# Query weights through four buffers, and a triangle inversion in 64-column blocks

## The chip, the cores and the metric

One core of a Trainium2 chip runs the kernel; the metric is the time of one execution on the device, in microseconds. The core has TensorE (PE; its weight loads are listed as PEld), VectorE (DVE), ScalarE (ACT), GpSimd (POOL) and SyncE (SP), each with its own queue of instructions that it works off in order; they wait for one another by semaphores. SyncE and GpSimd issue the DMAs.

## The reference, cut to what matters

One inference step of a one-layer decoder for two groups of tokens that share all weights: a prompt of 512 tokens and 8 samples of 8 tokens. All is float32.

```python
h = rmsnorm(x, g1) * (1 + sc1) + sh1          # the shifts and gates are silu(c) @ w_ada
proj = h @ w_in                               # 1024 -> 512 (S5) + 1792 (RWKV-7)
y_s5 = s5_mixer(proj[..., :512])              # diagonal state space, gelu, gated
y_rw = rwkv7_mixer(proj[..., 512:])           # 8 heads of 64: S = S*w - (S kk) (kk*a)^T + v k^T, y = S r
x = x + ga1 * (concat(y_s5, y_rw) @ w_out)
h = rmsnorm(x, g2) * (1 + sc2) + sh2
q = h @ w_q                                   # 8 heads of two halves of 64
s1, s2 = q_1 . keys1, q_2 . keys2             # 128 scores per half
idx, gate = softmax over the top 16 of (top 16 of s1) + (top 16 of s2)
ff = sum_k gate_k * gelu(u_tab[idx_k] . h) * v_tab[idx_k]    # 16384 experts, 128 per token
y = rmsnorm(x + ga2 * ff)
```

The recurrence of the RWKV part is computed in chunks of 64 tokens. Within a chunk that needs the inverse of a unit triangular 64 x 64 matrix for each head (8 x 8 blocks for the samples).

## The kernel before

Tokens are cut into five tiles: tile 0 holds the 64 sample tokens, tiles 1 to 4 hold 128 prompt tokens each, and they are worked in the order 1, 2, 3, 0, 4 (ORDER). Every tile passes through these stages, each of them a Python generator:

- front: the elementwise part of the RWKV mixer and the inversion. A prompt tile has two chunks of 64 tokens, a chunk 8 heads; heads lie in pairs, one on partitions 0 to 63 and one on 64 to 127. For each chunk, LT holds four such pairs as 128 x 128 matrices whose off-diagonal blocks are zero. The inverse grows by doubling: Dm and DT (the inverse and its transpose) begin as identities; on each of five levels TensorE forms LT x Dm (L1029), ScalarE evicts it (L1031), TensorE multiplies it with DT in two ways (L1037, L1041), and VectorE copies the blocks of that level into Dm and DT under a mask (L1042, L1043; masks in lev).
- back: the chunk recurrence with state S0, and the group norm.
- select: output projection with w_out (8 loads, L1230, matmuls L1232), norm, query projection with w_q (8 loads of 512 KB, one per head, L1270, matmuls L1272), and the products with the keys (loads L1276, matmuls L1286 and L1288). All these weights and two rows of modulation (ga1, sh2) go through one pool tag, "w", of two buffers.
- pick: the top 16 on VectorE (L1308 to L1312 on scores, L1335 to L1339 on candidates). For tiles 1, 2 and 3 (DENSE) it ends with three transposes on TensorE that put the chosen indices and gates into dib and dix (L1381 to L1385).
- gbuild, for the three dense tiles: 32 "quads" of four tokens each make one-hot factors (oh L1490 and ab L1497 on VectorE, ab L1494, L1495, L1500 on ScalarE, ab L1502 on GpSimd), multiply them (L1505), and ScalarE evicts the result into Gst (L1506). After four quads Gst is stored to Gd in HBM.

After all that comes the dense part: 128 blocks, each of a first product (pd, L1520, 24 matmuls) of 128 experts' u rows with 384 tokens, gelu, a multiplication with the gates Gr that are read back from Gd (wf, L1603), and a second product with the v rows (po, L1623, 18 matmuls). Beside it GpSimd gathers u and v rows for the tokens of tiles 0 and 4 (L1448), and VectorE reduces them.

Before all stands phase 1, the input projection and the S5 mixer; its end, with the rest of the conditioning product (ada, matmuls L303), is woven with the front of tile 1. Generators are advanced in turn (weave), and a scheduler then sets the order on each engine from priorities and its own estimate of times, so an edit in one stage can move instructions of all. The dense part's first loads are held until the last keys have been issued (kld).

Of the kernel before, what the change touches and what calls it, by code (L numbers as in the profile page):

```python
# [6 lines left out]
F32 = mybir.dt.float32  # L7
I32 = mybir.dt.int32
U32 = mybir.dt.uint32
U8 = mybir.dt.uint8  # L10
# [32 lines left out]
def layout(x):  # L43
# [60 lines left out]
    out["lev"] = np.stack(lv, 1).astype(np.float32)  # L104
# [73 lines left out]
class Kernel:  # L178
# [13 lines left out]
    B2 = {"r": 7, "l": 8, "b": 7, "s": 5}  # L192
# [658 lines left out]
    def open_rwkv(self):  # L851
# [11 lines left out]
        lev = wp.tile([128, 12, 128], U8)  # L863
# [21 lines left out]
        self.LTs = []  # L885
        for i in range(2):
            lt = wp.tile([128, 4, 128], F32, name="lt%d" % i)
            G.memset(lt, 0.0)
            self.LTs.append(lt)
        for q in range(0, 12, 6):  # L890
            lf = self.t4([6, 128])
            SY.dma_start(lf, I["lev"][:, q:q + 6])
            G.tensor_copy(lev[:, q:q + 6], lf)
# [12 lines left out]
    def front(self, ti):  # L906
# [84 lines left out]
        id4 = ident[:, None, :].to_broadcast([128, 4, 128])  # L991
        yield

        def lm(i):
            return self.lev[:, i, None, :].to_broadcast([128, 4, 128])
        cd = []
        for c in range(nch):
            gp = [ps([128, 4, 128], "r"), ps([128, 4, 128], "r")]
            for j in range(4):
                for hf in range(2):  # L1000
                    sl = slice(64 * hf, 64 * hf + 64)
                    T.matmul(gp[hf][:, j, :], BK[sl, c, j, :], AR[sl, c, j, :], start=True, stop=True)
            MG = t4([2, 4, 128])
            LT = self.LTs[c]
            for hf in range(2):
                sl = slice(64 * hf, 64 * hf + 64)
                V.tensor_tensor(MG[:, hf], gp[hf], gm[:, None, :].to_broadcast([128, 4, 128]), op=OP.mult)
                {"G": G.tensor_copy, "V": V.tensor_copy, "S": S.copy}[self.LTE[hf]](LT[sl, :, sl], MG[sl, hf, :, 0:64])
                gl = G.tensor_copy(MG[sl, hf, :, 0:64], AR[sl, c, :, 0:64])
            Dm = t2([4, 128])  # L1010
            DT = t2([4, 128], "l")
            S.copy(Dm, id4)
            S.copy(DT, id4)
            cd.append((MG, LT, Dm, DT))
            yield
        for MG, LT, Dm, DT in cd:
            pl = ps([128, 4, 128], "r")
            for j in range(4):
                T.transpose(pl[:, j, :], LT[:, j, :], ident)
            V.copy_predicated(Dm, lm(0), pl)  # L1020
            V.copy_predicated(DT, lm(1), LT)
        yield
        nl = 3 if smp else 6
        for l in range(1, nl):
            Bs = []
            for MG, LT, Dm, DT in cd:
                pb = ps([128, 4, 128], "r")
                for j in range(4):
                    T.matmul(pb[:, j, :], LT[:, j, :], Dm[:, j, :], start=True, stop=True)  # L1029
                Bm = t2([4, 128])  # L1030
                S.copy(Bm, pb)  # L1031
                Bs.append(Bm)
            yield
            for (MG, LT, Dm, DT), Bm in zip(cd, Bs):
                p2 = ps([128, 4, 128], "r")
                for j in range(4):
                    T.matmul(p2[:, j, :], Bm[:, j, :], DT[:, j, :], start=True, stop=True)  # L1037
                if l < nl - 1:
                    p1 = ps([128, 4, 128], "r")
                    for j in range(4):  # L1040
# [5 lines left out]
        self.rs[ti] = (AR, BK, [(MG, DT) for MG, LT, Dm, DT in cd], rk, vS, WL, gs)  # L1046

    def back(self, ti):
# [37 lines left out]
        for c in range(nch):  # L1086
            (MG, DT), (UV, BN) = cd[c], ub[c]
# [39 lines left out]
            for j in range(4):  # L1127
                T.matmul(pu[:, j, :], DT[:, j, :], Xs[:, j, :], start=True, stop=True)
# [75 lines left out]
    def select(self, ti):  # L1204
# [30 lines left out]
        ga1 = self.ws.tile([128, D], F32, name="ga1", tag="w", bufs=2)  # L1235
        self.mod(ga1, 0, smp)
        sh2 = self.ws.tile([128, D], F32, name="sh2", tag="w", bufs=2)
# [37 lines left out]
        keys = self.ws.tile([128, 8, 128], F32, name="keys", tag="w", bufs=2)  # L1275
# [463 lines left out]
```

## Time and profile before

| | |
|---|---|
| time, median of 3 runs (lowest, highest) | 1947.14 us (1943.68, 1952.03) |
| the profiled execution's own time | 1944.17 us |
| its span | 1942.4 us, 30575 instructions |
| TensorE | 1815.2 us busy (93%), 11183 matmuls |
| VectorE | 1533.6 us (79%) |
| ScalarE | 817.1 us (42%) |
| GpSimd | 676.0 us (35%) |
| mean granted clock of TensorE | 0.974 |
| DMA | 514.09 MB, mean 265 GB/s |

The shares are means over stages with different limits. The dense part fills the span from about 850 us on, with TensorE full; before it, up to that point, the stages of different tiles lie beside each other and the limit changes every 50 us or so. Times in the rows below are microseconds from the start of the span.

### The profile page before, as it was taken

The numbers are of one execution on the slowest core, as the hardware profiler recorded it, in microseconds if no ns is written. First come the engines' busy times: TensorE is split into PE (matmuls) and PEld (weight loads), VectorE is DVE, ScalarE is ACT, GpSimd is POOL, SyncE is SP. The second block draws the span as 40 slices with busy tenths as digits, with TensorE's granted clock in tenths as the row PEclk, the third lists the DMA queues.
The fourth block names the chain that finished last, engine by engine and source line by source line (L and its number), as shares of the span: only waits on it lengthen the run. The fifth ranks groups of instructions, "written<-read, shape, count | busy, mean of one in ns | idle before, by whom it ended". The sixth has DMA issues, their size and how long they took to land.

```text
span 1942.4 us, 30575 instructions
## 1 busy us (share of the span) xinstructions
PE 1815.2 (93%) x11183; PEld 1573.6 (81%) x11183; DVE 1533.6 (79%) x3117; ACT 817.1 (42%) x1494; POOL 676.0 (35%) x543
## 2 busy tenths in 40 slices
PE   8899998999979888689999999999999999999994
PEld 6699666877759686679999988899999999999993
DVE  7968435478797979399988877798888878888998
ACT  4232515525765788434333333433333333333332
POOL 0000201001262244313454434365444444544555
PEclk9899999989999999899999999999999999999998
DMA  8524653434345576789899998899999999999995
GB/s 330 152 86 103 220 181 104 142 123 152 126 163 185 190 255 241 282 281 311 299 372 354 351 348 321 272 383 352 341 350 321 349 337 344 331 343 349 326 316 200
DMA packets 203366, 514.09 MB, mean 265 GB/s; under 512 B 26248, under 2 KB 88840, under 8 KB 199120
## 3 DMA queue, kind: packets, MB, share of 16 engines
q1 hardware_dynamic: 147632, 309.74, 46.2%
q0 software_dynamic: 55584, 202.40, 28.7%
q8 instruction: 88, 1.44, 0.3%
q14 instruction: 62, 0.51, 0.1%
HBM read 471.28 MB, written 39.62 MB: 263 GB/s over the span
## 4 chain that ended last, share of the span: by engine, by line
PE 68%; DVE 13%; DMA 6%; ACT 5%; issue 5%; POOL 3%; SPq 0%; POOLq 0%; DVEq 0%; ACTq 0%
PE po L1623 23%; PE pd L1520 23%; PE par L329 4%; POOL gr L1448 3%; PE pas L1272 2%; DMA wq<-w_q 2%; PE par L1029 2%; PE par L1037 1%; PE pag L303 1%; PE pas L1232 1%; PE par L1041 1%; DVE oh L1490 1%; DMA gr<-v_tab,ei 1%; DVE idxu L1309 1%; PE pas L792 1%
## 5 line engine op out<-in xcount | busy, mean ns | idle before, releaser
L1448 POOL DMA_INDIRECT gr<-u_tab,ei x192 | 246.4, 1284 | 310.3 <-DVE scr L1453 256.7
L1448 POOL DMA_INDIRECT gr<-v_tab,ei x192 | 255.4, 1330 | 275.7 <-DVE acc L1463 240.3
L1520 PE MATMUL pd<-dh,uh 128*128 128x384 f32 x1024 | 344.7, 337 | 4.0 <-ACT wf L1601 3.1
L1520 PE MATMUL pd<-dh,ul 128*128 128x384 f32 x1024 | 344.8, 337 | 2.2 <-DVE ul L1517 2.2
L1520 PE MATMUL pd<-dl,uh 128*128 128x384 f32 x1024 | 343.6, 336 | 0.0
L1463 DVE SCALAR_TENSOR_TENSOR acc<-gr,act,acc 128x1024 f32<-128x1024 f32 x190 | 245.3, 1291 | 4.2 <-DMA gr<-v_tab,ei 2.4
L1516 ACT CAST uh<-ur 128x1024 fp32r<-128x1024 f32 x128 | 134.5, 1051 | 269.7 <-PE pd L1520 265.2
L1623 PE MATMUL po<-vl,wh 128*128 128x512 f32 x768 | 237.3, 391 | 1.2 <-DVE vl L1619 1.2
L1623 PE MATMUL po<-vh,wl 128*128 128x512 f32 x768 | 236.6, 390 | 0.0
L1453 DVE SCALAR_TENSOR_TENSOR scr<-gr,h 128x1024 bf16<-128x1024 f32 x192 | 233.8, 1218 | 1.3 <-DMA gr<-u_tab,ei 0.2
L1606 ACT CAST wh<-wf 128x384 fp32r<-128x384 f32 x128 | 65.9, 515 | 334.6 <-PE po L1623 310.8
L1623 PE MATMUL po<-vh,wh 128*128 128x512 f32 x768 | 200.3, 396 | 4.9 <-ACT vh L1618 4.4
L1517 DVE TENSOR_TENSOR ul<-ur,uh 128x1024 fp32r<-128x1024 f32 x128 | 156.4, 1222 | 61.4 <-ACT uh L1516 61.2
L1520 PEld LDWEIGHTS pd<-dh,uh 128*128 128x128 f32 x1024 | 192.7, 188 | 12.1 <-ACT wf L1601 4.9
L1520 PEld LDWEIGHTS pd<-dl,uh 128*128 128x128 f32 x1024 | 192.7, 188 | 5.2
L1520 PEld LDWEIGHTS pd<-dh,ul 128*128 128x128 f32 x1024 | 192.6, 188 | 3.7 <-DVE ul L1517 3.4
L1619 DVE TENSOR_TENSOR vl<-vr,vh 128x1024 fp32r<-128x1024 f32 x128 | 156.2, 1220 | 21.4 <-ACT vh L1618 21.3
L1623 PEld LDWEIGHTS po<-vl,wh 128*128 128x128 f32 x768 | 143.8, 188 | 32.6 <-DVE vl L1619 2.1
L1623 PEld LDWEIGHTS po<-vh,wl 128*128 128x128 f32 x768 | 144.1, 188 | 31.5 <-DVE wl L1607 0.4
L1623 PEld LDWEIGHTS po<-vh,wh 128*128 128x128 f32 x768 | 141.0, 188 | 33.4 <-ACT vh L1618 10.0
L1618 ACT CAST vh<-vr 128x1024 fp32r<-128x1024 f32 x128 | 134.5, 1051 | 46.7 <-PE po L1623 34.8
L1502 POOL TENSOR_TENSOR ab<-oh,dix 128x512 f32<-128x512 bf16 x72 | 88.2, 1230 | 150.2 <-DVE oh L1490 65.7
(472 smaller groups left out, 3135.8 us busy)
## 6 DMA issues: line engine op xcount, KB each, us to landing
ur<-u_t SPq DMA_DIRECT2D x128, 512.0 KB, 6.8
vr<-v_tab SPq DMA_DIRECT2D x128, 512.0 KB, 6.4
Gd<-Gst SPq DMA_DIRECT2D x24, 1024.0 KB, 4.8
Gr<-Gd SPq DMA_DIRECT2D x16, 1536.0 KB, 17.2
wo<-w_out SPq DMA_DIRECT2D x40, 512.0 KB, 4.5
wq<-w_q SPq DMA_DIRECT2D x40, 512.0 KB, 4.3
wt<-w_ada SPq DMA_DIRECT2D x32, 512.0 KB, 4.4
wr<-w_in SPq DMA_DIRECT2D x18, 512.0 KB, 6.7
```

Source lines behind the costliest of these rows:

```text
L329: mm = self.nc.tensor.matmul(p, w[:, k, :], h[:, k, c:c + 288], start=(k == 0 and i == 0), stop=(k == KB - 1 and i == 2))
L1448: G.indirect_dma_start(out=r, out_offset=None, in_=I[tab], in_offset=bass.IndirectOffsetOnAxis(ap=ei[:, k:k + 1], axis=0))
L1453: V.scalar_tensor_tensor(scr, r, 1.0, h2, op0=OP.mult, op1=OP.mult, accum_out=act[:, k:k + 1])
L1463: V.scalar_tensor_tensor(acc, r, act[:, k:k + 1], acc, op0=OP.mult, op1=OP.add)
L1502: G.tensor_tensor(A, oh, bc(self.dix[:, 1]), op=OP.mult)
L1516: nc.scalar.copy(uh, ur)
L1517: self.mark = nc.vector.tensor_tensor(ul, ur, uh.bitcast(F32), op=OP.subtract).ins
L1520: nc.tensor.matmul(pa, u[:, k, :], h[:, k, :], start=(k == 0 and i == 0), stop=(k == KB - 1 and i == 2))
L1606: S.copy(wh, wf)
L1618: S.copy(vh, vr)
L1619: V.tensor_tensor(vl, vr, vh.bitcast(F32), op=OP.subtract)
L1623: T.matmul(outs[2 * d + n], w[:, d * 128:(d + 1) * 128], v[:, n * 512:(n + 1) * 512], start=(b == 0 and i == 0), stop=(b == 127 and i == 2))
```

## The change

All of w_out, ga1, sh2, w_q and the keys get four buffers (tag "w", bufs=4). The room comes from the inversion, which no longer works on 128 x 128 matrices with zero blocks but on the 64 x 64 blocks alone, stacked on the two halves of the partitions: LT is one tile [128, 2, 4, 64] in place of two of [128, 4, 128], the masks lev are 64 columns wide, and the pool t2l has 6 buffers in place of 8. Both chunks of a prompt tile now go through each step together: one step is 16 products of 64 x 64 (8 for the samples), one eviction and one masked copy of [128, 8, 64].

```diff
-    B2 = {"r": 7, "l": 8, "b": 7, "s": 5}
+    B2 = {"r": 7, "l": 6, "b": 7, "s": 5}
...
-        lev = wp.tile([128, 12, 128], U8)
+        lev = wp.tile([128, 12, 64], U8)
...
-        for i in range(2):
-            lt = wp.tile([128, 4, 128], F32, name="lt%d" % i)
-            G.memset(lt, 0.0)
-            self.LTs.append(lt)
...
+        self.LT = wp.tile([128, 2, 4, 64], F32, name="LT")
...
+        def quads(out, a, b):
+            for u in range(m):
+                for hf in range(2):
+                    sl = slice(64 * hf, 64 * hf + 64)
+                    T.matmul(out[sl, u, :], a[sl, u, :], b(sl, u), start=True, stop=True)
...
         for l in range(1, nl):
-            Bs = []
-            for MG, LT, Dm, DT in cd:
-                pb = ps([128, 4, 128], "r")
-                for j in range(4):
-                    T.matmul(pb[:, j, :], LT[:, j, :], Dm[:, j, :], start=True, stop=True)
-                Bm = t2([4, 128])
-                S.copy(Bm, pb)
-                Bs.append(Bm)
-            yield
-            for (MG, LT, Dm, DT), Bm in zip(cd, Bs):
-                p2 = ps([128, 4, 128], "r")
-                for j in range(4):
-                    T.matmul(p2[:, j, :], Bm[:, j, :], DT[:, j, :], start=True, stop=True)
-                if l < nl - 1:
-                    p1 = ps([128, 4, 128], "r")
-                    for j in range(4):
-                        T.matmul(p1[:, j, :], DT[:, j, :], Bm[:, j, :], start=True, stop=True)
-                    V.copy_predicated(Dm, lm(2 * l), p1)
-                V.copy_predicated(DT, lm(2 * l + 1), p2)
+            pb = ps([128, m, 64], "r")
+            quads(pb, LT, lambda sl, u: Dm[sl, u, :])
+            Bm = t2([m, 64])
+            S.copy(Bm, pb)
+            yield
+            if l < nl - 1:
+                p1 = ps([128, m, 64], "r")
+                quads(p1, DT, lambda sl, u: Bm[sl, u, :])
+                V.copy_predicated(Dm, lm(2 * l), p1)
+            p2 = ps([128, m, 64], "r")
+            quads(p2, Bm, lambda sl, u: DT[sl, u, :])
+            V.copy_predicated(DT, lm(2 * l + 1), p2)
             yield
...
-                T.matmul(pu[:, j, :], DT[:, j, :], Xs[:, j, :], start=True, stop=True)
+                for hf in range(2):
+                    sl = slice(64 * hf, 64 * hf + 64)
+                    T.matmul(pu[sl, j, :], DT[sl, j, :], Xs[sl, j, :], start=True, stop=True)
...
-            wo = self.ws.tile([128, D], F32, name="wo", tag="w", bufs=2)
+            wo = self.ws.tile([128, D], F32, name="wo", tag="w", bufs=4)
...
-                wq = self.ws.tile([128, KB, 128], F32, name="wq", tag="w", bufs=2)
+                wq = self.ws.tile([128, KB, 128], F32, name="wq", tag="w", bufs=4)
```

(ga1, sh2 and the keys likewise.) The order of instructions changes on every engine. TensorE, one and a half levels of the inversion of tile 4, before (t2r and t2l are Dm, DT and the evicted product; wq are the query weights of tile 3):

```order
L1029 MATMUL par<-t2r,lt_2401 128x128 x4
L1272 MATMUL pas<-t4s,wq 128x128 x8
L1505 MATMUL pag<-ab 128x128 x2
L1505 MATMUL pah<-ab 128x128 x3
L1029 MATMUL par<-t2r,lt_2403 128x128 x4
L1037 MATMUL par<-t2l,t2r 128x128 x4
L1041 MATMUL par<-t2r,t2l 128x128 x4
L1272 MATMUL pas<-t4s,wq 128x128 x5
```

And in the changed kernel (L997 is the line of the 64 x 64 products, L1268 that of the query product):

```order
L997 MATMUL par<-t2r,LT 64x64 x16
L1268 MATMUL pas<-t4s,wq 128x128 x13
L997 MATMUL par<-t2r,t2l 64x64 x16
L997 MATMUL par<-t2l,t2r 64x64 x16
L1268 MATMUL pas<-t4s,wq 128x128 x6
```

The two chunks no longer alternate; what stands between a product and the ones that need its eviction is now a run of 13 or 6 query matmuls. SyncE, the loads of the fifth selection, before:

```order
L1270 DMA wq<-w_q 128x1024
L1245 DMA x1d<-t4s 128x1024
L1508 DMA Gd<-Gst 128x2048 x2
L1253 DMA h2d<-t4s 128x1024
L1270 DMA wq<-w_q 128x1024
L1508 DMA Gd<-Gst 128x2048 x2
L1270 DMA wq<-w_q 128x1024 x2
L1508 DMA Gd<-Gst 128x2048
L1270 DMA wq<-w_q 128x1024 x4
L1276 DMA keys<-keys 128x1024
L1513 DMA ur<-u_t 128x1024
L1575 DMA Gr<-Gd 128x24x128
```

And in the changed kernel:

```order
L1266 DMA wq<-w_q 128x1024 x3
L1241 DMA x1d<-t4s 128x1024
L1504 DMA Gd<-Gst 128x2048 x2
L1249 DMA h2d<-t4s 128x1024
L1266 DMA wq<-w_q 128x1024
L1504 DMA Gd<-Gst 128x2048
L1266 DMA wq<-w_q 128x1024 x4
L1272 DMA keys<-keys 128x1024
L1509 DMA ur<-u_t 128x1024 x3
L1504 DMA Gd<-Gst 128x2048 x6
L1611 DMA vr<-v_tab 128x1024 x2
L1504 DMA Gd<-Gst 128x2048
```

Three query loads stand ahead of the store of x1 in place of one, and seven of the gate matrices' 24 stores now stand behind the last keys, where there was none; the read of the gates (Gr, L1571) follows them, two rows further. TensorE where the last keys' products (L1288) meet the dense part, before:

```order
L1505 MATMUL par<-ab 128x128 x4
L1505 MATMUL pag<-ab 128x128 x4
L1505 MATMUL pah<-ab 128x128 x4
L1272 MATMUL pas<-t4s,wq 128x128 x48
L1288 MATMUL pas<-keys,t4s 128x128 x16
L1520 MATMUL pd<-dh,uh 128x384
L1520 MATMUL pd<-dl,uh 128x384
```

And in the changed kernel (L1501 is the product of gbuild, L1284 that of the keys, L1516 the first dense product):

```order
L1268 MATMUL pas<-t4s,wq 128x128 x32
L1284 MATMUL pas<-keys,t4s 128x128 x8
L1501 MATMUL pag<-ab 128x128 x3
L1501 MATMUL par<-ab 128x128 x2
L1284 MATMUL pas<-keys,t4s 128x128 x8
L1501 MATMUL par<-ab 128x128 x2
L1501 MATMUL pah<-ab 128x128
L1501 MATMUL pag<-ab 128x128 x4
L1501 MATMUL pah<-ab 128x128 x3
L1501 MATMUL par<-ab 128x128 x12
L1501 MATMUL pag<-ab 128x128 x4
```

Rows of this kind go on, and the first row of L1516 comes 11 rows further. Of the 96 quads of gbuild, 37 stood behind the third set of index transposes (L1381 to L1383) before, and 46 do now; behind the last keys' products there were none and are 22.

## Rows read from the trace of the kernel before

**Rows 1.** Chain of waits in the dense part: start us, us, what

```profile
890.41 4.18 PE pd L1520 x24
894.59 4.12 PE po L1623 x18
```

**Rows 2.** One stretch, PE alone at L1520 and L1623: length, busy (count), clock, DMA

```profile
825.00:890.41 65.41, 33.44 (x169) 0.97 0.82 273
825.00:890.41 65.41, 22.16 (x90) 0.97 0.82 273
```

**Rows 3.** ScalarE in order of time: start us, us, engine, line, op, tiles

```profile
507.52 0.27 ACT L1384 CAST dib<-pas 128x128 bf16<-128x128 f32 x1
...
732.75 0.29 ACT L1384 CAST dib<-pas 128x128 bf16<-128x128 f32 x1
...
804.57 0.58 ACT L1506 COPY Gst<-pah 128x512 f32<-128x512 f32 x1 [0.31 <-PE pah L1505]
```

**Rows 4.** Chain of waits in the fifth selection

```profile
800.10 5.64 DMA wq<-w_q
805.78 2.07 PE pas L1272 x16
...
807.86 3.58 DMA wq<-w_q
...
813.57 7.08 DMA wq<-w_q
...
824.33 3.85 DMA keys<-keys
```

**Rows 5.** Stretches: length, busy PE, PEld, DVE, ACT, POOL (count), clock, DMA, GB/s

```profile
410.00:450.00 40.00, 37.60 (x210) 26.43 (x210) 39.41 (x232) 13.04 (x23) 1.51 (x2) 1.00 0.38 127
...
507.00:573.00 66.00, 54.99 (x386) 36.62 (x385) 65.56 (x257) 45.88 (x114) 33.85 (x25) 0.95 0.42 148
589.00:636.00 47.00, 46.67 (x415) 45.66 (x414) 36.20 (x84) 21.81 (x53) 9.19 (x9) 1.00 0.53 177
...
700.00:733.00 33.00, 29.73 (x258) 28.21 (x257) 18.46 (x28) 32.48 (x78) 15.05 (x12) 0.95 0.83 291
...
798.00:832.00 34.00, 22.82 (x187) 21.70 (x185) 1.91 (x11) 7.40 (x14) 5.54 (x6) 0.95 0.92 328
```

**Rows 6.** Chain of waits in the first and the fourth selection

```profile
388.39 6.43 DMA wq<-w_q
...
689.80 6.39 DMA wq<-w_q
...
708.28 6.91 DMA wq<-w_q
```

**Rows 7.** Chain: a step, the state product, a masked copy; last, L1138's weight loads (ns min/median/max)

```profile
595.95 0.89 PE par L1029 x8
...
321.92 0.61 PE par L1138 x16
...
421.53 0.63 DVE t2r L1042
...
L1138 PEld LDWEIGHTS par<-t4x,Sn x96: 129/135/136, 381.3 to 688.0; 64*64 64x64 f32 x96
```

**Rows 8.** The page's DMA issues: tiles, queue, count, KB each, us to landing

```profile
Gd<-Gst SPq DMA_DIRECT2D x24, 1024.0 KB, 4.8
Gr<-Gd SPq DMA_DIRECT2D x16, 1536.0 KB, 17.2
...
wt<-w_ada SPq DMA_DIRECT2D x32, 512.0 KB, 4.4
```

**Rows 9.** One stretch, evictions of gbuild (L1506) on ScalarE: length, busy (count)

```profile
733.00:806.00 73.00, 20.30 (x37) 0.91 0.66 240
```

**Rows 10.** VectorE by line: operation, tiles, count | busy us, mean ns | idle before

```profile
L1619 DVE TENSOR_TENSOR vl<-vr,vh 128x1024 fp32r<-128x1024 f32 x128 | 156.2, 1220 | 21.4 <-ACT vh L1618 21.3
...
L1312 DVE FIND_INDEX8 idxu<-vals,t2s 128x8 uint32<-128x128 f32 x72 | 19.9, 284 | 0.0
```

**Rows 11.** Gathers on GpSimd: ns min/median/max, first and last start us

```profile
L1448 POOL DMA_INDIRECT gr<-u_tab,ei x192: 932/1146/2146, 811.3 to 1575.4; - x192
...
L1448 POOL DMA_INDIRECT gr<-v_tab,ei x192: 932/1196/1979, 1025.4 to 1913.5; - x192
```

More of the change, by code (lines that the diff above doesn't have):

```diff
@@ L103, in layout @@
         lv += [low, low.T]
-    out["lev"] = np.stack(lv, 1).astype(np.float32)
+    lv = np.stack(lv, 1).astype(np.float32)
+    out["lev"] = np.concatenate([lv[:64, :, :64], lv[64:, :, 64:]], 0)
     rst = np.ones((128, 2, 512), np.float32)
@@ L884, in open_rwkv @@
         V.tensor_reduce(mb8, self.con[:, 3, 64:128].rearrange("p (b t) -> p b t", t=8), op=OP.max, axis=AX.X)
-        self.LTs = []
-        for i in range(2):
-            lt = wp.tile([128, 4, 128], F32, name="lt%d" % i)
-            G.memset(lt, 0.0)
-            self.LTs.append(lt)
[L890 to L893, printed above, removed]
+        self.LT = wp.tile([128, 2, 4, 64], F32, name="LT")
+        lf = self.t4([12, 64])
+        SY.dma_start(lf, I["lev"])
+        G.tensor_copy(lev, lf)
         self.lev, self.rst, self.W2, self.g2 = lev, rst, W2, g2
@@ L990, in front @@
         gm = con[:, 3 if smp else 2, :]
-        id4 = ident[:, None, :].to_broadcast([128, 4, 128])
+        m = 4 * nch
         yield
         def lm(i):
-            return self.lev[:, i, None, :].to_broadcast([128, 4, 128])
-        cd = []
+            return self.lev[:, i, None, :].to_broadcast([128, m, 64])
+        def quads(out, a, b):
[3 more added lines that the diff above has]
+                    T.matmul(out[sl, u, :], a[sl, u, :], b(sl, u), start=True, stop=True)
+        LT = self.LT.rearrange("p c j t -> p (c j) t")[:, :m]
+        Dm = t2([m, 64])
+        DT = t2([m, 64], "l")
+        S.copy(Dm, self.fold[:, None, :].to_broadcast([128, m, 64]))
+        S.copy(DT, self.fold[:, None, :].to_broadcast([128, m, 64]))
+        MGs = []
         for c in range(nch):
@@ L1007, in front @@
                 V.tensor_tensor(MG[:, hf], gp[hf], gm[:, None, :].to_broadcast([128, 4, 128]), op=OP.mult)
-                {"G": G.tensor_copy, "V": V.tensor_copy, "S": S.copy}[self.LTE[hf]](LT[sl, :, sl], MG[sl, hf, :, 0:64])
+                {"G": G.tensor_copy, "V": V.tensor_copy, "S": S.copy}[self.LTE[hf]](LT[sl, 4 * c:4 * c + 4, :], MG[sl, hf, :, 0:64])
                 gl = G.tensor_copy(MG[sl, hf, :, 0:64], AR[sl, c, :, 0:64])
[L1010 to L1014, printed above, removed]
-            yield
-        for MG, LT, Dm, DT in cd:
-            pl = ps([128, 4, 128], "r")
-            for j in range(4):
-                T.transpose(pl[:, j, :], LT[:, j, :], ident)
-            V.copy_predicated(Dm, lm(0), pl)
-            V.copy_predicated(DT, lm(1), LT)
+            MGs.append(MG)
+            yield
+        pl = ps([128, m, 64], "r")
+        quads(pl, LT, lambda sl, u: ident[sl, sl])
+        V.copy_predicated(Dm, lm(0), pl)
+        V.copy_predicated(DT, lm(1), LT)
         yield
@@ L1024, in front @@
         for l in range(1, nl):
[L1025 to L1043 removed]
+            pb = ps([128, m, 64], "r")
+            quads(pb, LT, lambda sl, u: Dm[sl, u, :])
+            Bm = t2([m, 64])
+            S.copy(Bm, pb)
+            yield
+            if l < nl - 1:
[5 more added lines that the diff above has]
+            V.copy_predicated(DT, lm(2 * l + 1), p2)
             yield
         self.gl[ti] = gl.ins
[L1046 removed]
+        self.rs[ti] = (AR, BK, (MGs, DT), rk, vS, WL, gs)
     def back(self, ti):
@@ L1086, in back @@
         for c in range(nch):
-            (MG, DT), (UV, BN) = cd[c], ub[c]
+            MG, (UV, BN) = cd[0][c], ub[c]
+            DT = cd[1][:, 4 * c:4 * c + 4, :]
             S0 = self.S0
@@ L1234, in select @@
                 yield
-        ga1 = self.ws.tile([128, D], F32, name="ga1", tag="w", bufs=2)
+        ga1 = self.ws.tile([128, D], F32, name="ga1", tag="w", bufs=4)
         self.mod(ga1, 0, smp)
-        sh2 = self.ws.tile([128, D], F32, name="sh2", tag="w", bufs=2)
+        sh2 = self.ws.tile([128, D], F32, name="sh2", tag="w", bufs=4)
         self.mod(sh2, 1, smp)
@@ L1274, in select @@
             S.copy(qT[:, 4 * q:4 * q + 4, :], pt)
-        keys = self.ws.tile([128, 8, 128], F32, name="keys", tag="w", bufs=2)
+        keys = self.ws.tile([128, 8, 128], F32, name="keys", tag="w", bufs=4)
         self.kld = SY.dma_start(keys, I["keys"])
```

1 line of the change is left out of this document (removed).

## The prediction

> **What bounds the kernel now.** I read the page first: TensorE is busy 93% of the span, so the question is where its columns are useful and where it waits. Then the chain of waits, in order of time. From 890 us on it is one unbroken alternation of two dense products, 4.18 and 4.12 us, 8.30 us for each of 128 blocks [rows 1]: 1062 us in which this change touches nothing. What can move is the moment from which this runs. At 890.41 us, 169 of the first product's matmuls and 90 of the second's had started [rows 2], which is 169/24 x 4.18 + 90/18 x 4.12 = 50.0 us of dense work. So before behaves as if the dense part had begun at 840.4 us and never paused. I call this the start; all terms below move it.
>
> Next I asked what the start waits for. The building of the three tiles' gate matrices (gbuild, 96 groups of four tokens, "quads") begins with the first index transposes at 507.5 us and ends with the last eviction at 804.57 + 0.58 = 805.2 us [rows 3]. The dense part does not follow at once, because the fifth selection is still reading its query weights: between 800 and 828 us the chain alternates 2.07 us of matmul for a head with waits of 5.64, 3.58, 7.08 us for the next weights, and 3.85 us for the keys [rows 4]. Meanwhile VectorE is busy 1.91 of 34 us and ScalarE 7.40 [rows 5]. That is the hole the change aims at: 35.2 us between the end of gbuild and the start. Further back the stretches differ, and rows 5 show it: 410 to 450 and 507 to 573 us belong to VectorE (39.4 of 40 and 65.6 of 66), 589 to 636 to TensorE (46.7 of 47), 700 to 733 to ScalarE (32.5 of 33).
>
> **The change part by part.** First the weights. With four buffers two further heads are asked for before the first is used, so a head needs 2.07 us of TensorE and a load can take four times that; I cost the three head waits and the keys' wait of the fifth selection at zero. In earlier selections the chain shows such waits of 6.43, 6.39 and 6.91 us [rows 6]. Of the first I take 5 us, as ScalarE's queue is close behind it; the other two stand where ScalarE is full with gbuild, so they are only worth it if gbuild can be left behind and paid later. The new order does that, so I take 13.3 us and charge the gbuild below. SyncE issues all loads in order: the third head now stands ahead of the store of x1, which waits for later work anyway, and the stores of gbuild stand behind runs of three or four loads instead of one or two. Each such store waits for its own four evictions, so I cost that at nothing, and at up to 5 us where a load must wait for its buffer.
>
> Second the inversion, a set of products being one step for a tile. Before, a step for both 64-row chunks is twice four full products, 2 x 0.89 = 1.78 us [rows 7]. Now it is 16 products of 64 x 64. No row has this step, but the state product L1138 has its exact form, rows and outputs alternating between the halves: eight in 0.61 us [rows 7], so 16 take 1.22 us. That is the value. The lower end is 0.89 us (a product streams half the columns of a full one, 0.11 us, and two run at a time), the upper 16 x 0.135 = 2.16 us, if each had to wait out the 135 ns load of its weights [rows 7]. VectorE's masked copies and ScalarE's evictions go from two per step to one; a masked copy lasts 0.63 us [rows 7].
>
> The Trainium skill speaks against this. Its page "TensorEngine Tiling (Array Packing)", section "Gotcha 1: PSUM Pressure", says that different row tiles cannot access the same PSUM bank at the same time, and the new products put both halves into one bank. By that rule the set costs the upper end, 2.16 us, more than before. The trace does not agree so far: the eight products of L1138 also fill both halves of one bank, and start 76 ns apart.
>
> Where a set is cheaper counts only where TensorE or VectorE holds the chain. Third tile, 410 to 450 us: about 11 masked copies of 0.62 us become half, 3.4 us. 450 to 459 us: 9 of the old half-sets on the chain (8.7 us by 0.89 to 1.13) become 4.5 sets of 1.22, 3.2 us. The sample tile, half as wide: 1.5 us. Fifth tile, 589 to 636 us: 28 half-sets of 0.89 = 24.9 us become 14 sets of 1.22 = 17.1, 7.8 us. The order confirms that this stretch stays full: runs of 6 to 13 head products stand between a set and the set that needs its eviction. The first tile, before 290 us, I cost at 0: there TensorE alternates with the conditioning product, whose loads of 4.4 us [rows 8] go through two buffers of their own and are not changed; up to 5 us if it was TensorE after all.
>
> So the moment at which the third dense tile's indices are ready (732.75 us before [rows 3]) comes earlier by 5 + 3.4 + 3.2 + 1.5 + 7.8 + 13.3 = 34 us: 699 us. What is late next is gbuild. In the order 46 quads stand behind those transposes, where 37 did, and 22 of them behind the last keys' products where none did. Before, the 37 [rows 9] took from 732.75 to 805.2, 1.96 us each with all that ScalarE did beside them. 46 x 1.96 = 90 us, gbuild ends at 789. Behind it the stored gates must land and be read back, 4.8 + 17.2 us [rows 8], and one multiplication and the split, some 2.5 us: the second product starts 25 us after gbuild. Three blocks of the first product, 3 x 4.18 = 12.5 us, are done in that time, so the start is 789 + 12.5 = 802: 39 us earlier. VectorE must pass 87 small operations of the fifth pick before that multiplication (at most 0.28 us each, at some 0.2 us in the mean 17 us) and four splits of v and u rows of 1.2 us [rows 10], some 22 us; they fit in the 25 us, and cost up to 8 if not.
>
> A second route does not need the selections to run as I computed. If gbuild takes its 297.7 us from the first indices to the end as before, and only the first indices come earlier, by the terms before 507 us (5 + 3.4 + 3.2 + 1.5 = 13), it ends at 792 and the start is 804.6: 36 us. I take the second, 36 us. Profiled execution: 1944.2 - 36 = 1908; it is 3 us under the median of the three runs, so the forecast for a median is 1947.1 - 36 = 1911.
>
> **The rivals.** One, slower: gbuild is starved by the re-ordering. Over its whole length a quad took 297.7/96 = 3.1 us, since VectorE mixes it with the picks; only the last 37 went at 1.96. If the 46 left go at 3.1, the start is 699 + 143 + 12.5 = 854.5, 14 us later than before: 1961. It turns slower from 2.8 us per quad. For it: VectorE is full in 507 to 573. Against it: the last 22 quads have no selection beside them any more. Two, the small products do not overlap: 2.16 us per set instead of 1.22, 14 + 4.5 + 2.5 sets, 20 us given back: 1931. For it speaks that no row has the step itself, against it L1138. The rule of "Gotcha 1: PSUM Pressure" on the Trainium skill's page on tiling would bring this about. Three, the gathers end the kernel rather than TensorE: the first is issued at 811.3 us and the last at 1913.5 [rows 11], and TensorE's last block is 15 us later than an unbroken run from 840.4 would give. They start when gbuild leaves GpSimd, so some 19 us earlier instead of 36: 1928. Four, more: the waits hidden behind the two full engines vanish as well, 55 us: 1892. Five, nothing: gbuild at 2.6 to 2.9 us per quad eats what the selections give; within 10 us of 1947.
>
> **How the numbers follow.** About 10 us, 0.5%, is what a measurement of this kernel can tell from none. Forecast (20 to 50 us): 0.50. Small products in sequence: 0.10. Gathers: 0.12. More: 0.08. Nothing: 0.10. Slower: 0.10. Faster is 0.50 + 0.08 + 0.10 + 0.12 = 0.80, less 0.02 for small products that cost more than 2.16 us; the same is 0.10 + 0.02 = 0.12, slower 0.10. The range from 1888 to 1946 takes in the forecast, both weaker cases, and part of "nothing".
>
> **What would show it.** Right: no wait for query weights of more than 2 us on the chain; a set at L997 of about 1.2 us; indices of the third dense tile near 700 us; the last gate eviction near 790; the second dense product 25 us after it. Wrong: sets of 2 us; gbuild's quads at 2.5 us or more behind the indices; TensorE idle for more than 15 us behind the last gate product; gathers holding the last 100 us of the chain.

## The result, and the profile after

The changed kernel takes 1922.38 us (median of 4 runs, 1920.37 to 1927.33) against 1947.72 us for the kernel before on the same chip: ratio 0.9892, 95% interval 0.9868 to 0.9916, so 25.3 us or 1.1% faster. The forecast was 1911, the range 1888 to 1946. The profiled execution took 1922.7 us.

The dense part is what it was [rows 1]. The chain of waits of the changed kernel, from the end of gbuild into the dense part (start us, us, what):

```profile
804.77 1.09 ACT Gst L1502 x2
...
805.87 7.57 DMA Gd<-Gst
...
813.55 14.93 DMA Gr<-Gd
...
829.71 6.54 PE po L1619 x18
836.25 4.19 PE pd L1516 x24
840.44 4.12 PE po L1619 x18
```

Still 8.30 us for a block. When this begins is read as before [rows 2], from a stretch that ends where a first product begins, TensorE at L1516, then at L1619 (length, busy PE and PEld with counts, clock, DMA share, GB/s):

```profile
760.00:895.57 135.57, 48.24 (x264) 46.09 (x264) 0.94 0.79 280
...
760.00:895.57 135.57, 32.90 (x127) 25.29 (x128) 0.94 0.79 280
```

264/24 x 4.18 + 127/18 x 4.12 = 75.05 us of dense work were behind it, so the start is 895.57 - 75.05 = 820.5 us, where it was 840.4. These 19.9 us are the change: the profiled execution is 21.4 us shorter. ScalarE in order of time at the first indices, the third indices and the last eviction, which answers to [rows 3]:

```profile
475.41 0.27 ACT L1380 CAST dib<-pas 128x128 bf16<-128x128 f32 x1
...
704.04 0.27 ACT L1380 CAST dib<-pas 128x128 bf16<-128x128 f32 x1
...
805.25 0.60 ACT L1502 COPY Gst<-pah 128x512 f32<-128x512 f32 x1
```

The indices come 32.1 and 28.7 us earlier, but gbuild ends at 805.8 us, where it ended at 805.2. All that was won is the hole behind it: 840.4 - 805.2 = 35.2 us before, 820.5 - 805.8 = 14.7 us now. The fifth selection, whose waits were the hole [rows 4], is done 30 us before gbuild. So the dense part followed the selection before (its last scores were evicted at 832.5 us) and follows gbuild now. The selection's part of the chain:

```profile
723.03 3.52 DMA wq<-w_q
726.56 1.28 DVE t4s L1236 x2
...
755.29 7.15 PE pas L1268 x64
...
762.66 7.15 PE pas L1268 x64
769.81 1.64 PE pas L1284 x16
```

Eight heads go at one go, without a wait. The load of 3.52 us that the chain names before them does not hold a head: what it releases is VectorE's multiplication with ga1 (L1236), and VectorE was busy up to that moment. What TensorE waited for weights in the selections shows in the view of its waits from 290 to 850 us (total us, times, longest us), first the kernel before:

```profile
PE pas L1272 <- DMA wq<-w_q: 11.7, 7, 4.6
...
PE pas L1232 <- DMA wo<-w_out: 3.8, 2, 3.5
...
PE pas L1288 <- DMA keys<-keys: 2.2, 1, 2.2
...
PE pas L1286 <- DMA keys<-keys: 0.2, 1, 0.2
```

and the changed kernel, where it is the only such line:

```profile
PE pas L1228 <- DMA wo<-w_out: 6.6, 1, 6.6
```

The inversion of the fifth tile on the chain of the changed kernel (32 records are one step of 16 products; a step of 8 records was four full products in [rows 7]):

```profile
585.88 1.08 PE par L997 x32
586.96 3.10 PE pas L1268 x26
590.06 2.01 PE par L997 x64
```

A step takes 1.00 to 1.08 us at full granted clock. And the stretches that answer to [rows 5] and [rows 9] (length, busy PE, PEld, DVE, ACT, POOL with counts, clock, DMA share, GB/s):

```profile
475.40:611.00 135.60, 113.93 (x1093) 88.33 (x1094) 114.69 (x339) 84.88 (x204) 50.40 (x44) 0.90 0.44 152
575.00:615.00 40.00, 40.00 (x623) 37.58 (x624) 21.35 (x76) 18.13 (x44) 5.52 (x7) 0.96 0.59 194
704.00:771.00 67.00, 52.67 (x344) 44.14 (x344) 50.47 (x179) 45.09 (x119) 23.18 (x19) 0.90 0.63 229
771.00:806.00 35.00, 29.78 (x220) 28.19 (x219) 25.39 (x100) 33.69 (x87) 16.11 (x13) 0.90 0.51 197
```

The evictions of gbuild alone (L1502, length, busy, count):

```profile
704.00:805.90 101.90, 25.36 (x46) 0.90 0.59 218
```

46 quads behind the third indices at 2.21 us each. In the last 35 us ScalarE is full, 33.7 of 35; between 575 and 615 us TensorE is full and VectorE idle for 18.7 of 40 us, in which it stood above all behind these (waits of VectorE, total us, times, longest us):

```profile
DVE t2r L1033 <- PE par L997: 9.1, 2, 6.6
DVE vals L1304 <- ACT t2s L1286: 5.1, 1, 5.1
```

The longest wait of VectorE lies behind the third indices. From 759.2 to 771.2 us it stands at the split of the dense part's first u rows (ul) behind ScalarE's cast of them (uh), and ScalarE at that cast behind their load (waits from 704 to 806 us):

```profile
DVE ul L1513 <- ACT uh L1512: 12.0, 1, 12.0
ACT uh L1512 <- DMA ur<-u_t: 7.1, 1, 7.1
```

In both queues operations of gbuild stand behind these first operations of the dense part, whose load left SyncE only behind the keys', at 764.9 us. In the kernel before there is no such wait behind the third indices. TensorE was at the query products for most of that time (755 to 771 us), so how much of the 12 us gbuild lost by it is open.

### The profile page after: what moved, and what is told of

It is laid out like the page before. It is cut to its first block, busy times and chain, and to the rows that moved or that the text cites. A ratio compares the mean times of both kernels' runs of the same rounds, so it can differ in the third digit from the quotient of the medians.

```text
span 1921.0 us, 32712 instructions
## 1 busy us (share of the span) xinstructions
PE 1772.8 (92%) x12299; PEld 1527.8 (80%) x12299; DVE 1508.1 (79%) x3073; ACT 801.0 (42%) x1466; POOL 683.0 (36%) x540
## 3 DMA queue, kind: packets, MB, share of 16 engines
q0 software_dynamic: 55584, 202.40, 28.7%
## 4 chain that ended last, share of the span: by engine, by line
PE 62%; DVE 10%; ACT 2%; DMA 1%; issue 1%; POOL 1%; POOLq 0%; DVEq 0%; ACTq 0%; SPq 0%
PE po L1619 27%; PE pd L1516 27%; PE pas L1268 3%; DVE oh L1486 1%; PE par L1501 1%; DVE ab L1493 1%; DMA Gr<-Gd 1%; PE pas L1228 1%; PE pag L1501 1%; PE pah L1501 1%; PE par L997 0%; DVE vals L1304 0%; DVE idxu L1305 0%; DVE idxu L1308 0%; DVE t2s L1306 0%
## 5 line engine op out<-in xcount | busy, mean ns | idle before, releaser
L1444 POOL DMA_INDIRECT gr<-v_tab,ei x192 | 261.0, 1359 | 274.6 <-DVE acc L1459 233.5
L1444 POOL DMA_INDIRECT gr<-u_tab,ei x192 | 251.6, 1310 | 274.0 <-DVE scr L1449 250.4
L1516 PE MATMUL pd<-dh,uh 128*128 128x384 f32 x1024 | 343.8, 336 | 4.8 <-ACT wf L1597 4.8
L1516 PE MATMUL pd<-dh,ul 128*128 128x384 f32 x1024 | 343.8, 336 | 0.0
L1516 PE MATMUL pd<-dl,uh 128*128 128x384 f32 x1024 | 343.2, 335 | 0.0
L1619 PE MATMUL po<-vl,wh 128*128 128x512 f32 x768 | 239.0, 392 | 0.6 <-DVE vl L1615 0.6
L1619 PE MATMUL po<-vh,wl 128*128 128x512 f32 x768 | 236.8, 390 | 0.0
L1619 PE MATMUL po<-vh,wh 128*128 128x512 f32 x768 | 202.2, 398 | 15.2 <-ACT wh L1602 7.7
L1516 PEld LDWEIGHTS pd<-dh,uh 128*128 128x128 f32 x1024 | 192.3, 188 | 11.1 <-ACT wf L1597 5.8
L1516 PEld LDWEIGHTS pd<-dl,uh 128*128 128x128 f32 x1024 | 192.2, 188 | 6.0 <-issue 0.8
L1516 PEld LDWEIGHTS pd<-dh,ul 128*128 128x128 f32 x1024 | 192.1, 188 | 0.4
L1619 PEld LDWEIGHTS po<-vh,wh 128*128 128x128 f32 x768 | 141.8, 189 | 43.3 <-ACT vh L1614 12.8
L1619 PEld LDWEIGHTS po<-vl,wh 128*128 128x128 f32 x768 | 144.5, 189 | 33.1 <-DVE vl L1615 1.4
L1619 PEld LDWEIGHTS po<-vh,wl 128*128 128x128 f32 x768 | 144.2, 188 | 31.2
L1614 ACT CAST vh<-vr 128x1024 fp32r<-128x1024 f32 x128 | 134.4, 1050 | 21.2 <-DMA vr<-v_tab 15.3
```

The costliest lines, as they stand in the source:

```text
L1444: G.indirect_dma_start(out=r, out_offset=None, in_=I[tab], in_offset=bass.IndirectOffsetOnAxis(ap=ei[:, k:k + 1], axis=0))
L1516: nc.tensor.matmul(pa, u[:, k, :], h[:, k, :], start=(k == 0 and i == 0), stop=(k == KB - 1 and i == 2))
L1614: S.copy(vh, vr)
L1619: T.matmul(outs[2 * d + n], w[:, d * 128:(d + 1) * 128], v[:, n * 512:(n + 1) * 512], start=(b == 0 and i == 0), stop=(b == 127 and i == 2))
```

## The experiments

The theories at the outset. W: the weights' buffers bring the gain. I: the inversion brings it. B: only both together. Later M: the dense part starts behind the later of the fifth selection and gbuild, and what counts is how the order shares the engines between them; S: ScalarE's rate holds the end of gbuild; D: VectorE's standing behind TensorE does. Times in us; the last keys are the last eviction of scores, the quads are evictions of gbuild behind the third indices and behind the last keys, and the start is worked out as above, at 80 us behind the first second product. The kernels were timed on several chips; each ratio is to the kernel before on the same chip, where that took 1943 to 1948 us.

| kernel | third indices | last keys | gbuild's end | quads behind | start | median | ratio to before (95%) |
|---|---|---|---|---|---|---|---|
| before | 732.8 | 832.5 | 805.2 | 37, 0 | 840.4 | 1947.72 | |
| changed | 704.0 | 775.8 | 805.8 | 46, 23 | 820.5 | 1922.38 | 0.9892 (0.9868-0.9916) |
| inv_two | 731.4 | 818.0 | 821.0 | 32, 4 | 837.0 | 1940.17 | 0.9978 (0.9959-0.9997) |
| inv_three | 691.1 | 782.0 | 791.4 | 48, 9 | 809.6 | 1911.77 | 0.9841 (0.9813-0.9870) |
| old_two_room | 734.0 | 822.0 | 824.1 | 35, 3 | 830.8 | 1934.04 | 0.9956 (0.9931-0.9981) |
| old_three | 728.2 | 815.4 | 826.2 | 46, 11 | 852.0 | 1959.54 | 1.0083 (1.0061-1.0106) |
| old_four | 725.5 | 803.5 | 835.7 | 48, 25 | 849.1 | 1955.17 | 1.0052 (1.0036-1.0068) |
| four_even | 706.5 | 789.0 | 800.7 | 46, 13 | 817.6 | 1922.54 | 0.9896 (0.9877-0.9915) |
| four_gfirst | 715.1 | 798.9 | 800.9 | 40, 4 | 817.2 | 1920.66 | 0.9897 (0.9870-0.9925) |
| four_lightB | 705.4 | 782.7 | 798.9 | 46, 16 | 814.5 | 1914.38 | 0.9855 (0.9829-0.9880) |
| four_split | 706.7 | 779.0 | 809.0 | 46, 23 | 816.0 | 1916.69 | 0.9857 (0.9832-0.9883) |
| four_serial | 714.3 | 788.4 | 813.1 | 45, 21 | 833.8 | 1936.67 | 0.9956 (0.9938-0.9974) |
| four_front | 701.0 | 776.4 | 798.0 | 45, 19 | 815.5 | 1920.29 | 0.9883 (0.9857-0.9909) |
| three_both | 687.8 | 770.3 | 786.3 | 48, 16 | 794.8 | 1913.00 | 0.9850 (0.9828-0.9871) |

**The two parts, taken apart.** The inversion alone, and with three buffers:

```diff
-            wo = self.ws.tile([128, D], F32, name="wo", tag="w", bufs=4)
+            wo = self.ws.tile([128, D], F32, name="wo", tag="w", bufs=2)
```

(and so for ga1, sh2, wq, keys; 3 in the other kernel.) Expected of two:

> The changed kernel with the weights back in two buffers: only the inversion in 64-column blocks. Theory W (the weights bring most of it): the selections wait for their query weights again, the fifth one for 15 us or more, the first indices come at 495 to 505 us instead of 475, gbuild ends near 800 with the hole behind it back; 1938 to 1945 us. Rival I (the inversion brings it, since a step costs fewer instructions on all three engines): first indices within 10 us of 475, time within 6 us of the changed kernel, 1917 to 1928. Rival B (both are needed, neither does anything alone): within 5 us of before, 1943 to 1953.

Expected of three:

> The changed kernel with the weights in three buffers. Theory W with one more load ahead (about 4 us of cover per buffer): most of the waits gone, a third to two thirds of the way between two and four, 1925 to 1934 us. Rival I: as the changed kernel, 1919 to 1927. If the last buffer does nothing because loads take 4 us and a head 2 us, also 1919 to 1927, but then the kernel with two buffers tells W and I apart.

Then the buffers alone, in the kernel before. Room for them had to come from elsewhere, so there is a control with that room taken and two buffers:

```diff
-    B2 = {"r": 7, "l": 8, "b": 7, "s": 5}
+    B2 = {"r": 7, "l": 6, "b": 7, "s": 5}
...
-    AB = 9
+    AB = 7
```

> Control: the kernel before, weights in two buffers, but with 6 buffers for evicted products of the inversion instead of 8 and 7 for gbuild's factors instead of 9, the room that four weights' buffers need. What the room costs by itself: 0 to 10 us over before, 1947 to 1958, under every theory.

The same with four buffers for the weights:

> The kernel before with the old inversion and four buffers for the weights, in the room of the control. Theory W: 12 to 25 us under the control, first indices 15 to 25 us earlier than the control. Rival I: within 5 us of the control. Rival B: within 5 us of the control.

and with three:

> The kernel before with the old inversion and three buffers for the weights, in the room of the control (1934 us with two, 1955 with four). If three is a better number than four or two whatever the inversion: 15 to 25 us under the control, 1909 to 1920. Theory E (with the old inversion the engines are full where the loads would let go, so buffers give nothing): within 8 us of the control, 1928 to 1942. If more buffers hurt in proportion: 1942 to 1950.

What was measured is none of the simple cases. The inversion alone gives 0.2%, its first indices come at 505.1 us (507.5 before): theory I is out. Its time, 1940, is what theory W had, but the hole is not back as W had it: the start is 837.0 - 821.0 = 16.0 us behind gbuild, which itself ends 15 us later than in the changed kernel. So the hole and gbuild's end are not two terms that can be added; what four buffers give here is a start 16.5 us earlier. The buffers alone make the kernel slower, by 21 us (four) and 25 us (three) against the control: theory W is out. Together they give 1.1% with four and 1.6% with three, which had been expected between two and four. That is theory B, but sharper: without the new inversion the buffers are a loss. The control is itself 0.4% faster than before, though it only loses room (0 to 10 us slower had been expected); so a mere change of order moves this kernel by some 10 us, and differences of that size between the kernels here are not put down to a cause without a row that shows it. No run holds the order fixed while the buffers change, so what the buffers give by their waits and what by the order that comes with them is not told apart.

The traces show where the loss comes from. In old_four the selections do come earlier than in the control, the first indices by 12.8 us, the last keys by 18.5; but 48 quads are left behind the third indices where the control has 35, and gbuild ends 11.6 us later. The chain of old_four:

```profile
833.63 2.06 ACT Gst L1506 x4
835.71 8.01 DMA Gd<-Gst
...
843.91 13.98 DMA Gr<-Gd
```

In old_three gbuild ends 2 us later than in the control, and the start 21 us later. Its chain:

```profile
834.56 17.28 DMA Gr<-Gd
...
853.08 6.90 PE po L1623 x18
```

The read of the gates leaves SyncE 8.4 us behind gbuild's end, which is nothing lost: in the control it is 8.5. The read then takes 17.3 us, and the second product begins 18.5 us behind the read's issue, in the control 10.8; that is 7.7 us. The first product has three blocks of lead in both. But the second product takes 6.9 us in place of 4.1 (mean granted clock 0.61 in that stretch, 1.00 in the control), and TensorE then pauses, mostly behind a load of u rows that lasts 15.3 us on the chain, which moves the start by another 9 us within the 80 us (and by 5 more behind them). Together these make the 21 us. Why the loads take so long there, the traces do not show.

**The price of a step of 64 x 64 products.** The same products, one half of the partitions after the other instead of alternating:

```diff
-            for u in range(m):
-                for hf in range(2):
-                    sl = slice(64 * hf, 64 * hf + 64)
+            for hf in range(2):
+                sl = slice(64 * hf, 64 * hf + 64)
+                for u in range(m):
```

> The changed kernel, with the 64 x 64 products of one step in another sequence: all of the lower half, then all of the upper half, in place of alternating halves. If alternation is what lets two run at a time: a step of 16 products takes 1.8 us or more where it takes 1.05 now, the inversion's TensorE time rises by some 50%, and the time by 5 to 15 us, 1928 to 1938. If the halves overlap anyhow or the step is paid by its weight loads: 1.0 to 1.2 us per step, 1918 to 1927 (the order behind it also changes a little: 43 and 20.75 quads behind the third indices and the last keys).

A step on the chain of this kernel:

```profile
588.52 1.82 PE par L997 x32
```

1.82 us, or 114 ns for a product, against 1.00 to 1.08 us, 63 to 68 ns, when the halves alternate, both at full granted clock. A full product takes 0.89/4 = 0.22 us [rows 7] for 128 columns, so one of 64 columns would take 111 ns by itself. The serial order is at that, the alternating one well below: two do run at a time, and only if neighbours in the queue are of different halves. It costs 14 us between the medians (12 by the ratios), as the first expectation had it. In the sum of TensorE's busy time for one of the three products of a level (L997, busy us, mean ns), the changed kernel, then this one:

```profile
L997 PE MATMUL par<-t2r,LT 64*64 64x64 f32 x672 | 24.4, 221 | 3.1 <-DVE t2r L1033 3.1
```

```profile
L997 PE MATMUL par<-t2r,LT 64*64 64x64 f32 x672 | 40.6, 223 | 0.0
```

The mean of one record is the same, 221 and 223 ns: that number does not tell whether two run beside each other, the chain does.

**What holds gbuild's end.** First the order: the fifth selection without its priority, then also with gbuild raised.

```diff
-    PO, GO, SO, RO, FO = {}, {}, {4: 4000}, {}, {}
+    PO, GO, SO, RO, FO = {}, {}, {4: 0}, {}, {}
```

> The changed kernel, but the fifth selection without its priority of 4000 over the rest. In the order 12.75 quads of gbuild stand behind the last keys instead of 22.5, and 46 behind the third indices as before. Theory M (the dense part starts when the later of two chains is done, the fifth selection and gbuild; four buffers let the selection run away from gbuild, which then ends 30 us behind it): the selection ends 10 to 15 us later than 776, gbuild 10 to 15 earlier than 806, the start of the dense part near 810; 1908 to 1915 us. Rival S (the last quads go at the speed of ScalarE whatever stands between them): gbuild ends at 806 as now, 1919 to 1925. Rival W (an early selection is what pays): later by what the selection loses, 1928 to 1936.

```diff
+    PO, GO, SO, RO, FO = {}, {3: 2000, 4: 2000}, {4: 0}, {}, {}
```

> The changed kernel, gbuild of the second and third dense tile raised by 2000 and the fifth selection's priority taken away: 40 quads behind the third indices, 3 behind the last keys. Theory M: gbuild ends at 785 to 795, the selection at 795 to 805, and the start is some 8 us behind the selection as in the kernel before (832 to 840): 805 to 815, 1906 to 1916 us. Rival S: gbuild's end stays at 800 or more and the selection is late too, 1922 to 1932. Rival W: 1930 to 1940.

Both let the selection end later, by 13 and 23 us, and gbuild earlier, but only by 5. The start gains 3 us and the time nothing that can be measured. Theory M is right that the selection has time to give (23 us of it cost nothing), and wrong that gbuild would take it. Next ScalarE's load:

```diff
-                if q % 4 in self.BA:
+                if q % 4 in (self.BA[:1] if d == 2 else self.BA):
```

> The changed kernel, with the factor B of the third dense tile's gbuild built on ScalarE for one quad in four instead of two (VectorE makes the others, as it does for the rest already): ScalarE loses 8 times 2.3 us of its 79 us behind the third indices, VectorE gains 8 times 0.85 us. Rival S: gbuild ends 10 to 18 us earlier, 1905 to 1914 us. Theory M alone, with TensorE's order as the limit: the same within 5 us, 1918 to 1926. If VectorE is the limit: 3 to 7 us slower.

The stretch from the third indices to gbuild's end, of the changed kernel and of this one:

```profile
704.00:805.80 101.80, 82.25 (x560) 72.13 (x560) 75.66 (x278) 78.73 (x205) 39.29 (x32) 0.90 0.59 218
```

```profile
705.40:798.90 93.50, 78.09 (x565) 68.44 (x565) 81.70 (x263) 65.09 (x165) 41.12 (x32) 0.96 0.64 237
```

13.6 us taken from ScalarE bring gbuild's end 6.9 us forward, where theory S wanted 10 to 18, and the start 6.0; the time is 0.4% less, with intervals of the two ratios that just overlap. Two other things changed in that stretch: the wait for the first u rows fell from 12.0 to 3.2 us on VectorE and from 7.1 to 3.5 on ScalarE, and the granted clock rose from 0.90 to 0.96. That ScalarE holds part of the stretch is what its full last 35 us suggest, but this run does not show it by itself. Then VectorE's standing:

```diff
-    PO, GO, SO, RO, FO = {}, {}, {4: 4000}, {}, {}
+    PO, GO, SO, RO, FO = {}, {}, {4: 4000}, {}, {2: 1000}
```

> The changed kernel, with the front of the fifth tile (its inversion) raised by 1000 over the sample tile's selection. In the changed kernel VectorE stands 9 us behind a masked copy whose products lie behind runs of 13 query products. Theory D (gbuild's end is VectorE's work plus the time it stands behind other engines): it stands less than 4 us there, gbuild ends at 795 to 800 instead of 806, 1911 to 1918 us. Rival S (only ScalarE's rate behind the third indices counts): gbuild's end as it was, 1919 to 1926. Rival: the selection pays what the inversion gains, same within 4 us.

gbuild ends at 798.0, as theory D had it, but not for its reason: VectorE's standing between 575 and 615 us rose from 9.1 to 13.8 us. Its wait for the dense part's first u rows fell, from 12.0 to 7.8. The start is 5 us earlier, the time the same within the intervals. Theory D stays unproved.

That wait goes with gbuild's end in part only. VectorE has 10.6 us of it in four_serial and 12.6 in four_split, where gbuild ends late, 3.2 to 7.8 in four_lightB, four_front and three_both, and none in inv_three, four_even and four_gfirst; but four_even, without it, gains just 5 us. No run takes it away alone.

**The way from gbuild to the dense part.** The first read of the gates in two transfers:

```diff
-            SY.dma_start(t.rearrange("p g n t -> p g (n t)"),
-                         self.Gd[:, :, g * GBL * TG:(g + 1) * GBL * TG].rearrange("g p x -> p g x"))
+            tr, w = t.rearrange("p g n t -> p g (n t)"), slice(g * GBL * TG, (g + 1) * GBL * TG)
+            for lo, hi in ((0, 16), (16, 24)) if g == 0 else ((0, 24),):
+                SY.dma_start(tr[:, lo:hi], self.Gd[lo:hi, :, w].rearrange("g p x -> p g x"))
```

> The changed kernel; the first read of the gate matrices is two transfers, one for the first two dense tiles' gates (1 MB) and one for the third's (0.5 MB), so that only the small one stands behind the last store. If the read's bytes set the 24 us from the last eviction to the second dense product (store 7.6, read 14.9): the read behind the last store takes 6 to 8 us, the product comes 7 to 9 us sooner, 1912 to 1917 us. If a read's fixed cost does, or VectorE's pick behind it: within 3 us of the changed kernel, 1919 to 1925.

The second product comes 17.9 us behind gbuild's end instead of 23.9. Why not sooner is on its chain:

```profile
822.85 0.37 DVE posu L1332 x2
823.23 1.16 DVE ul L1513
...
825.75 0.48 DVE wf L1600
...
826.31 0.52 ACT wh L1603
...
826.87 3.36 PE po L1620 x7
```

The read has left the chain; VectorE's operations of the fifth pick stand there now. Besides, the last store left SyncE 2.6 us behind gbuild's end, behind two loads of v rows, where it had left at once. The start is 4.5 us earlier; gbuild itself ended 3 us later than in the changed kernel. The time is 0.35% less, with intervals that overlap.

**Three of those with an earlier start, together.** Three buffers, the lighter ScalarE and the split read:

> The new inversion with three buffers for the weights, the lighter share of factors on ScalarE for the third dense tile, and the first read of the gates in two transfers. If the three gains add up (10.6, 7 and 5 us under the changed kernel): 1898 to 1905 us. If three buffers have already taken what lighter ScalarE gives (gbuild's end at 791 there): 1904 to 1911. If the order that the scheduler finds decides (14.5 quads behind the last keys in place of 9): 1908 to 1918.

The start is where it should be if gains add up, 794.8 us, 15 us before that of inv_three. But the last second product ends at 1888.6 us, against 1889.3 for inv_three: the 15 us are given back in the dense part. Between 1078 and 1368 us TensorE stood behind the cast of v rows (total us, times, longest us),

```profile
PE po L1620 <- ACT vh L1615: 12.7, 11, 2.0
PE pd L1516 <- ACT wf L1598: 2.9, 3, 1.3
```

where the changed kernel, in the stretch of the same length from its own corresponding block, has

```profile
PE po L1619 <- ACT vh L1614: 3.1, 3, 1.1
PE pd L1516 <- ACT wf L1597: 0.6, 1, 0.6
```

Both gather streams run there, and the DMA engines are 98% busy at 360 GB/s between 1200 and 1285 us; so they are in the changed kernel between 1245 and 1330 us (98%, 363 GB/s), where TensorE does not pause, so that this share alone explains nothing. The gathers had begun at 798.8 us, 2.3 us before those of inv_three, and not 15. What exactly makes the v rows late was not tried. The fastest version found is inv_three, 0.5% faster than the changed kernel (0.9841 against 0.9892; the intervals just touch at 0.987); three_both is not faster than it.

## Why the prediction was right, and where it was not

Direction and range held, and the larger part of the mechanism: the wait of the dense part for the fifth selection was there and has gone. The other part, an earlier end of gbuild, did not come. The size was 36 and is 25, in the profiled executions 36 and 21.4. Of the 36, the hole was to give 35.2 - 12.5 = 22.7 and gbuild's earlier end 13. The hole gave 20.5. gbuild's end gave -0.6. Step by step:

- **The weights.** The waits of the fifth selection's heads and keys, costed at zero, were zero, and TensorE's waits for weights in all selections fell from 17.9 to 6.6 us. For the first selection I took 5 us. The first x1 came 13.9 us earlier (343.0, from 356.9) and its last head's eviction 24.5 us. Most of that needs the buffers: in inv_two, which has two, the first indices are only 2.4 us earlier than before. Around the first heads the kernel before also had a lower clock than the changed one. Before, between the first heads and the first scores, then after:

```profile
383.50:410.00 26.50, 23.39 (x221) 21.61 (x222) 13.65 (x25) 5.05 (x14) 2.58 (x4) 0.81 0.39 117
```

```profile
368.60:385.00 16.40, 15.85 (x209) 14.08 (x209) 10.52 (x20) 6.53 (x14) 2.06 (x4) 1.00 0.69 235
```

  Which part the loads of w_out have in it, for which the buffers also count and which I had left out, no run tells apart.
- **The step of the inversion.** 1.22 us taken, 1.00 to 1.08 measured, well inside the bounds. The rival that the small products run in sequence is out for the order in which the kernel issues them, and is what four_serial shows for the other, at 1.82 us in place of the 2.16 of the rival. The rule of "Gotcha 1: PSUM Pressure" on the Trainium skill's page "TensorEngine Tiling (Array Packing)", that row tiles cannot access one PSUM bank at the same time, does not show here: both halves write one bank and take 63 to 68 ns each.
- **What the cheaper step is worth.** The 1.5 and 7.8 us for the sample tile and the fifth tile did not come: from the first to the second indices it took 135.6 us, where it took 128.3. TensorE is full from 575 to 615 us as I had it from 589 to 636, but VectorE idles more beside it (18.7 of 40 us, 10.8 of 47 before [rows 5]). Between the first and the second indices TensorE's busy time is 113.9 us in both kernels, though a step is cheaper; the mean granted clock there was 0.90, and 0.96 before. How much of the missing gain that is, no run tells apart. The third indices, forecast at 699, are at 704 by two errors that nearly cancel: 32 us instead of 13 before the first indices, -3 instead of 21 between the first and the third.
- **gbuild, the step that failed.** "46 x 1.96 = 90 us, gbuild ends at 789": the quads took 2.21 us, 101.8 us, and with the 5 us of later indices that is the end at 805.8. The 1.96 was the mean of a stretch in which the fifth selection's query products began only at 798 us [rows 9]; the 46 include 22 that stand beside the fifth selection, at 67/22 = 3.0 us each, and 24 beside a full ScalarE, at 35/24 = 1.46 us. Of the 67 us, VectorE stood 12.0 at the dense part's first u rows, a term that the prediction did not have. The second route, which I took, failed outright: gbuild from the first indices to its end was not 297.7 but 330.4 us. An earlier beginning does not bring an earlier end when the order leaves more for later. VectorE's work from 302 us (the first output projection of the kernel before) to gbuild's end is 388.0 us before and 381.3 after, its idle time 115.2 and 122.5. inv_three has 380.7 and 108.7: same work, less idle, and an end 14 us earlier. These sums are bookkeeping and do not show that VectorE holds the end; but the wait for the first u rows, 12.0 us, which inv_three does not have, is nearly as long as the 13.8 us by which the two idle times differ.
- **From gbuild to the dense part.** 25 us forecast, 829.7 - 805.8 = 23.9 measured; the lead of the first product 12.5 forecast, 829.7 - 820.5 = 9.2 measured. The three blocks of lead are there, as forecast. Of the missing 3.3 us, 2.4 are the second product itself, 6.54 us in place of 4.12 at a mean granted clock of 0.64, behind 7.7 us in which TensorE had stood; some 1 us is a pause 35 us later. VectorE's pick "fits in the 25 us" held for the changed kernel; four_split shows it on the chain, where the cover is shorter.
- **The rivals.** "Slower", quads starved by the order, decides from 2.8 us a quad; the changed kernel is at 2.21. Its sign is that of old_four: earlier selections, a later end of gbuild and a slower kernel, though at 2.30 us a quad (2.57 in the control), with 13 quads more. "Gathers" did not occur: TensorE's last block comes 16.5 us behind an unbroken run from the start, as it did before (16.0). In three_both, with its still earlier start, that block comes 31 us behind, for a reason left open. The 19 us of this rival are worked out from no row.

Left open: why the order with four buffers makes VectorE wait between 575 and 615 us and the order with three does not (four_front was to show it and moved the wait instead), and what the wait for the first u rows costs. A run that keeps the dense part's first cast and split behind gbuild on ScalarE and VectorE would tell.

## What to carry to other kernels

An earlier start of a stage is worth nothing if the work that ends last is merely left for later: cost the stage that ends last by what stands beside it in the new order, not by its old length shifted. Look there for the first operations of the next stage: one that waits for a load also holds what stands behind it in its engine's queue. More buffers change the order that a scheduler finds as well as the waits, so try the number (here three was better than four), with a control that takes the same room. And a pair of changes may gain where one alone loses and the other gives next to nothing, so a part that failed alone is worth a second look together with the one that makes room on the engines.

## What the runs showed of the hardware that was not expected

Sixteen float32 products of 64 x 64 take 1.00 to 1.08 us if neighbours in TensorE's queue lie on different halves of the partitions, and 1.82 us if eight of one half follow eight of the other, both at full granted clock; the mean duration of a single record (two for a product) in the trace is 221 to 223 ns in both.
